# Hybrid retention and S5 step on one core: later ties in the last stage, a later start of retention with joined visits, and the last partial sums added by DMA

## The chip, the cores and the metric

The kernel runs on one core of a Trainium2 chip. A core has a matrix engine (TensorE, here PE, with its weight loads shown apart as PEld), a vector engine (VectorE, DVE), an activation engine (ScalarE, ACT), GpSimd (POOL), a queue engine (SyncE, SP) and 16 DMA engines. Each engine works through its own queue in order. DMAs are issued from the queues of SP, ACT and POOL; an accumulating DMA (one that adds what it reads to what stands at its destination) is issued from POOL. The metric is device time in microseconds (us), the median of several executions. One further execution was recorded by the profiler, and all rows below come from it.

## The reference

One layer of a hybrid decoder, for a prompt of 1024 tokens and 8 sample tokens, in float32, model width 2048:

```python
h = rmsnorm(x, g_pre)
proj = h @ w_in                     # 2048 x 10240
q, k, v, za, ub, zb, ga, gb = split(proj)
ya, s_ret_new = retention(q, k, v, pos, s_ret)       # 8 heads of 128, chunks of 128
ya = (ya * silu(za)) @ w_pa
yb, s_re_new, s_im_new = s5(ub, ...)                 # diagonal state space, gelu, glu gate
yb = (yb * silu(zb)) @ w_pb
merged = sigmoid(ga) * ya + sigmoid(gb) * yb
out = merged @ w_out
return x + rmsnorm(out, g_post), s_ret_new, s_re_new, s_im_new
```

In retention every head has rotated q and k, a decaying state carried over chunks of 128 tokens, scores within a chunk, and a normalization over the head's 128 values. The sample tokens take one step of the same recurrence from a given state.

## The kernel before

**Products.** Activations lie transposed in SBUF, features on the partitions and the 1032 tokens along the free axis. Every float32 operand of a large product is split into a rounded part and a remainder, and a product of two such operands is three matmuls (high by high, high by low, low by high). From the input projection's third pair of row blocks on, the large products go by a Strassen-like scheme: a step (`s`) is a pair of output row blocks and two groups of four k tiles, and has seven products (`n` = 0 to 6) in place of eight. A product (number `g` = 7s + n) is 24 matmuls of 256 to 260 columns pairwise (`product`, L993), or in the out-projection 12 of 324. `prep` makes the weight forms two products ahead (sums on DVE by `add`, L85; the high part on ACT, L974; the remainder on DVE), `evac_st`, `evac_p` and `evac_o` take the sums out of PSUM into the tiles `p1`, `u2`, `u3` (shown as `p`, `u`) and `st`. The steps run in this order: the first part of the input projection, its second half (74 steps in all), the S5 gate (`glu`, 4 steps), the two gated projections `pa` and `pb` (8 each), and the out-projection in two halves of k, `o0` and `o1` (8 each), for tokens 384 to 1031. The scheme needs sums and differences of activation halves; these forms are loaded into `stg` tiles (`stage`, L932) and split (`unstage`, ACT L274 and DVE) by `transition` while the step before still runs.

**Order.** One program order is written out by hand, and a scheduler at compile time puts each engine's instructions into its queue: an instruction goes out when its operands are ready in that schedule, by program order among those that are ready. `tc.issue_after(ins)` holds what is traced in its block behind `ins` in the order of that engine alone on which `ins` runs. `anchor` holds the latest instructions of SP, ACT, DVE and PE. After every product `late_work(g)` runs what was put off with `at(g, ...)`, and `slot()` lets the first background generator of the queue `bg` go on to its next `yield`. One such turn is called a visit.

**Retention** is such a generator (`retention`, L1293). It is put into `bg` at the start of step `C0 + 12` of the input projection, when the pools of the stage before (`k2p`, for reordering the S5 output: tiles `yr`, `yo`) have been closed and the pool `ret` opened in their place. `ret_const` allocates its tiles, fills `mhalf` (-0.5, the exponent of a power that makes the reciprocal root) and loads tables. `head` (L1162) then takes a head in visits: the transposes of v and of the sample tokens' v, which goes out to `vs_d` (L1181) and comes back broadcast as `vb` (L1184); the transposes of k; the state pass, two visits of four matmuls each with four updates on DVE (L1197 to L1205); the sample state; the scores (L1218); the outputs (L1228, L1230); the sample output, a product on DVE and sums over partitions with the small matrices `sel` in two visits (L1239); statistics; the scaling; the transposes back (L1276) and of the sample rows (L1281), and the gating with za. `load_vk` loads the next head's v and k. Between two heads' outputs `mix` makes forms for `pa`.

**Gated projections.** In `pb` the result of a tile is multiplied by its gate (`gated`), and the partial sum that `pa` left in `pap_d` is added. For p = 0 and 1 this is an accumulating DMA into the tile (L1581), and the write to `mg_d` (L1582) is put off by `LAG` = 4 products. For p = 2 to 7 the partial sum is loaded beforehand into a tile `pp` on ACT's queue, DVE adds it, and the tile goes to `mg_d` at once (L1579). `forms_o` reads rows of `mg_d` (L1619) and makes the forms for the out-projection into `fo_d`; its `ld(2)` reads, among others, rows 6 or 14, its `ld(3)` rows 7 or 15.

**The last stage** (L1868 on) is the out-projection of tokens 0 to 383 the other way round, with the tokens on the partitions: three blocks of 128 tokens (c), four column groups of 512 (g), 16 k tiles, three matmuls each (L1874). It counts on in `now`. A group has three banks of PSUM; two of them are halves of one tile, `both_`. In the last group the first 11 k tiles go round the blocks, and then each block does its last five and is taken out by `evac_c`: a sum of squares on ACT (L1845), the product with the norm weights `gb` on DVE (L85), and for the last group the reciprocal root on POOL (L1854), the final scaling with the residual row added (L1857) and the writes of the result (L1858), one for blocks 0 and 1 and three for block 2. `gb` and the residual rows of block 0 (`x_of(0)`) are loaded at steps 9 and 20 of this stage, on POOL's queue, 1 MB each. Beside it run `split_m`, which splits the merged activations of the coming k tiles, and `rows_out`, the norm and the output of the other tokens.

Of the kernel before, what the change touches and what calls it, by code (L numbers as in the profile page):

```python
# [10 lines left out]
F32 = mybir.dt.float32  # L11
F32R = mybir.dt.float32r
I32 = mybir.dt.int32
AF = mybir.ActivationFunctionType
# [65 lines left out]
def emit(ctx, tc, I, O):  # L80
# [80 lines left out]
    rstd = const.tile([128, TOK], F32, name="rstd")  # L161
    warm = const.tile([128, 1], F32, name="warm")
    A.activation(warm, onesk, AF.Square)
    gpre = cload("g_pre", [128, KD])
# [71 lines left out]
    def misc():  # L236
        return banks_of["pms"].tile([128, 512], F32, name="misc")
# [895 lines left out]

    def ret_const():
        K["a"] = act.tile([128, 2, TOK], F32, name="a12")
        K["b"] = act.tile([128, 2, TOK], F32, name="a13")
        vT, kT = K["next"] = R("vT", [128, TOK]), R("kT", [128, TOK], 2)
        P.dma_start(vT, v_d[0])
        yield
        for n, shape in (("col", [128, 4, H]), ("mask", [128, 128])):  # L1140
            K[n] = rp.tile(shape, F32, name=n)
            P.dma_start(K[n], I[n])
        K["mhalf"] = rp.tile([128, 8], F32, name="mhalf")
        V.memset(K["mhalf"], -0.5)
        K["sel"] = rp.tile([128, 2, 32], F32, name="sel")
        P.dma_start(K["sel"].rearrange("p b c -> p (b c)"), I["sel"])
        for a in range(2):
            yield
            P.dma_start(kT[64 * a:64 * a + 64], kq_d[0, 0, a, 0:64])
        yield  # L1150
        yield
# [3 lines left out]
    def load_vk(h):  # L1155
# [4 lines left out]
        return vT, kT  # L1160

    def head(h):  # L1162
        col, mask, mhalf, sel = (K[n] for n in ("col", "mask", "mhalf", "sel"))
# [8 lines left out]
        for i in range(2):  # L1172
# [3 lines left out]
            A.copy(vt[:, 4 * i:4 * i + 4], ps.rearrange("p (c d) -> p c d", c=4))  # L1176
        ps = misc()
        T.transpose(ps[0:8, 0:128], vT[:, SEQ:TOK], ident)
        vs = R("vs", [128, 128])[0:8]
        V.tensor_copy(vs, ps[0:8, 0:128])  # L1180
        P.dma_start(vs_d[h].rearrange("(b d) -> b d", b=8), vs)  # L1181
        yield
# [11 lines left out]
        for i in range(2):  # L1194
            ps = misc()
            for c in range(4):
                T.matmul(ps[:, c * 128:(c + 1) * 128], kt[:, 4 * i + c, :], vt[:, 4 * i + c, :], start=True, stop=True)  # L1197
            for c in range(4):
                n = 4 * i + c
                o = ps[:, c * 128:(c + 1) * 128]  # L1200
                if n == 0:
                    V.tensor_copy(st[:, 0], o)
                else:
                    V.scalar_tensor_tensor(st[:, n], st[:, n - 1], gc, o, ALU.mult, ALU.add)
            yield  # L1205
        P.dma_start(O["retp"][h], st[:, 7])
# [30 lines left out]
        for i in range(2):  # L1237
            for b in range(4):
                T.matmul(ps[32 * b:32 * b + 32, 0:128], sel[:, i, :], pq[:, 4 * i + b], start=i == 0, stop=i == 1,  # L1239
                         tile_position=(0, 32 * b), skip_group_check=True)  # L1240
            if i == 0:
                yield
        ons = R("vs", [128, 128])
# [36 lines left out]
        ps = misc()  # L1280
        T.transpose(ps[:, 0:128], ons, ident)  # L1281
        eb = lambda t: t.rearrange("p (e b) -> p e b", e=2)
        mul(eb(oo[:, SEQ:TOK]), ps[:, 0:128].rearrange("p (b r) -> p r b", r=32)[:, 0:2], eb(za[:, SEQ:TOK]))
# [264 lines left out]
    def load_z(s, name):  # L1548
        kind, p = steps[s]
        r, c = AT[name]  # L1550
        zq[name] = zz_tile()
        A.dma_start(zq[name], {"glu": zy_d, "pa": sga_d, "pb": sgb_d}[kind][2 * p + r, :, HT * c:HT * c + HT])
        if kind == "pb" and p > 1:
            zq[name, "p"] = ppp.tile([128, HT], F32, name="pp")
            A.dma_start(zq[name, "p"], pap_d[2 * p + r, :, HT * c:HT * c + HT])
# [55 lines left out]
    def forms_o(kh, wait):  # L1611
# [14 lines left out]
        for n in range(wait):  # L1626
            yield
            if n == 1:
                ld(2)
# [213 lines left out]
    def evac_c(g, c, ps):  # L1843
# [8 lines left out]
        if g == 3:  # L1852
            V.scalar_tensor_tensor(r1, s4[:, 3:4], 1.0 / D, r1, ALU.mult, ALU.add)
            P.tensor_tensor(r3, r1, r2, ALU.pow)  # L1854
            for i, (a, b) in enumerate(((0, D),) if c < 2 else ((0, 1024), (1024, 1536), (1536, D))):
                z = flat(12 + c, "zc")[:, a:b]
# [5 lines left out]
    for g in range(4):  # L1862
        both_ = banks_of["pst"].tile([128, 2, 512], F32, name="acc")
        ps = [both_[:, 0, :], both_[:, 1, :], mmbank()]
        e = 11 if g == 3 else 13
        todo_ = [[(k, c) for c in range(3)] for k in range(e)] + [[(k, c) for k in range(e, KD)] for c in range(3)]
        for st in todo_:
# [9 lines left out]
            now[0] += 1  # L1877
            if now[0] == lim[0] + 9:
                P.dma_start(gb, bass.AP(tensor=I["g_post_row"].tensor, offset=I["g_post_row"].offset, ap=[[0, 128], [1, D]]))
            if now[0] == lim[0] + 20:  # L1880
                P.dma_start(x_of(0), I["xB"][0])
            if rest:
                with ExitStack() as after:
                    for ins in anchor.values():
                        after.enter_context(tc.issue_after(ins))
                    split_m(rest.popleft())
# [89 lines left out]
```

## Time and profile before

| | us |
|---|---|
| median of 3 executions | 2524.94 |
| lowest and highest of them | 2524.39, 2530.12 |
| the profiled execution | 2526.21 |
| its span, from the first to the last instruction | 2524.4 |

| engine | busy us | share of the span |
|---|---|---|
| PE | 2497.7 | 99% |
| PEld | 2449.6 | 97% |
| DVE | 2011.1 | 80% |
| ACT | 996.8 | 39% |
| POOL | 779.1 | 31% |

How rows of the profile are read: a timeline row gives the start, the duration, the engine, the line of the kernel, the operation, the names of output and inputs (`out<-in`), the shape and the number of like instructions drawn together; in brackets stands how long the engine was idle before it and what ended that. The row of a waits view names who waited for whom, the total, how often, and the longest. A row of the chain gives the start, the duration, the engine, the tile, the line and the count. A row of a window gives its length, the busy time and number of instructions of each engine, the clock that PE was granted, the busy share of the DMA engines and GB/s. Releasers are worked out from semaphores, and one wait for several is put down to the last.

### The profile page before, as it was taken

The numbers are of one execution on the slowest core, as the hardware profiler recorded it, in microseconds if no ns is written. First come the engines' busy times: TensorE is split into PE (matmuls) and PEld (weight loads), VectorE is DVE, ScalarE is ACT, GpSimd is POOL, SyncE is SP. The second block draws the span as 40 slices with busy tenths as digits, with TensorE's granted clock in tenths as the row PEclk, the third lists the DMA queues.
The fourth block names the chain that finished last, engine by engine and source line by source line (L and its number), as shares of the span: only waits on it lengthen the run. The fifth ranks groups of instructions, "written<-read, shape, count | busy, mean of one in ns | idle before, by whom it ended". The sixth has DMA issues, their size and how long they took to land.

```text
span 2524.4 us, 52842 instructions
## 1 busy us (share of the span) xinstructions
PE 2497.7 (99%) x20026; PEld 2449.6 (97%) x20026; DVE 2011.1 (80%) x4212; ACT 996.8 (39%) x1787; POOL 779.1 (31%) x1299
## 2 busy tenths in 40 slices
PE   9999999999999999999999999999999999999998
PEld 8999999999999999999999999999999999999976
DVE  7677789898898898768986766666897878989784
ACT  7143532333333333453334444435552422445532
POOL 0321223222322222223344434444332222433320
PEclk9999999999999999999999999999999999999999
DMA  5879865434434434787889888888888689956883
GB/s 195 282 234 289 231 170 143 139 121 137 131 117 138 135 120 128 244 207 202 223 228 253 225 235 223 211 220 248 270 288 282 226 241 314 304 191 163 220 298 134
DMA packets 242878, 527.59 MB, mean 209 GB/s; under 512 B 42832, under 2 KB 69664, under 8 KB 241856
## 3 DMA queue, kind: packets, MB, share of 16 engines
q0 software_dynamic: 106176, 310.76, 43.1%
q1 hardware_dynamic: 101536, 166.14, 21.1%
q10 hardware_dynamic: 34912, 47.31, 6.0%
q8 instruction: 158, 2.59, 0.4%
q14 instruction: 96, 0.79, 0.1%
HBM read 348.71 MB, written 175.37 MB: 208 GB/s over the span
## 4 chain that ended last, share of the span: by engine, by line
PE 88%; DVE 4%; DMA 3%; issue 3%; POOL 1%; ACT 1%; DVEq 0%; POOLq 0%; ACTq 0%; SPq 0%
PE acc L993 73%; PE acc L1874 4%; PE mm L228 2%; PE mm L229 2%; PE mm L227 2%; DMA u<-pt_d 1%; DMA wr<-in_w_in 1%; DVE u L85 1%; PE misc L825 1%; PE misc L824 1%; DMA wr<-in_w_outB 1%; PE misc L1218 1%; PE misc L1228 1%; PE misc L1197 1%; PE misc L775 1%
## 5 line engine op out<-in xcount | busy, mean ns | idle before, releaser
L993 PE MATMUL acc<-a,whib 128*128 128x256 f32 (+1 forms) x3816 | 629.7, 284 | 4.0 <-DVE u L85 2.3
L993 PE MATMUL acc<-a,whic 128*128 128x256 f32 (+1 forms) x3808 | 629.0, 284 | 2.9 <-DVE u L85 2.3
L993 PE MATMUL acc<-a,whia 128*128 128x256 f32 (+1 forms) x3800 | 627.3, 284 | 0.5 <-ACT whia L974 0.5
L993 PEld LDWEIGHTS acc<-a,whic 128*128 128x128 f32 x3808 | 525.1, 188 | 8.4 <-issue 2.8
L993 PEld LDWEIGHTS acc<-a,whib 128*128 128x128 f32 x3816 | 525.8, 188 | 7.0 <-ACT whia L974 3.9
L993 PEld LDWEIGHTS acc<-a,whia 128*128 128x128 f32 x3800 | 524.3, 188 | 2.7 <-issue 1.4
L993 PE MATMUL acc<-a,wloc 128*128 128x256 f32 (+1 forms) x1904 | 396.4, 283 | 0.4 <-DVE wloc L85 0.4
L993 PE MATMUL acc<-a,wlob 128*128 128x256 f32 (+1 forms) x1908 | 396.8, 283 | 0.0
L993 PE MATMUL acc<-a,wloa 128*128 128x256 f32 (+1 forms) x1900 | 395.2, 283 | 0.0
L993 PEld LDWEIGHTS acc<-a,wloc 128*128 128x128 f32 x1904 | 297.8, 188 | 1.3 <-DVE wloc L85 1.2
L993 PEld LDWEIGHTS acc<-a,wlob 128*128 128x128 f32 x1908 | 298.3, 188 | 0.2
L993 PEld LDWEIGHTS acc<-a,wloa 128*128 128x128 f32 x1900 | 297.1, 188 | 0.0
L974 ACT CAST whic<-wraw 128x512 fp32r<-128x512 f32 x148 | 92.0, 622 | 235.6 <-PE acc L993 157.9
L974 ACT CAST whib<-wraw 128x512 fp32r<-128x512 f32 x146 | 90.7, 622 | 228.7 <-PE acc L993 174.7
L974 ACT CAST whia<-wraw 128x512 fp32r<-128x512 f32 x146 | 90.7, 621 | 221.9 <-PE acc L993 158.9
L85 DVE TENSOR_TENSOR wraw<-wr 128x512 f32<-128x512 f32 x220 | 151.1, 687 | 2.6
L85 DVE TENSOR_TENSOR wloc<-wraw,whic 128x512 fp32r<-128x512 f32 x156 | 107.0, 686 | 50.4 <-ACT whic L974 39.8
L974 ACT CAST whib<-wr 128x512 fp32r<-128x512 f32 x111 | 68.9, 621 | 191.6 <-PE acc L993 155.1
L85 DVE TENSOR_TENSOR wloa<-wraw,whia 128x512 fp32r<-128x512 f32 x154 | 105.6, 686 | 48.2 <-ACT whia L974 32.7
L85 DVE TENSOR_TENSOR a<-stg,a 128x516 fp32r<-128x516 f32 (+1 forms) x224 | 136.2, 640 | 8.4 <-ACT a L274 7.9
L85 DVE TENSOR_TENSOR wlob<-wraw,whib 128x512 fp32r<-128x512 f32 x154 | 105.6, 686 | 46.4 <-ACT whib L974 35.4
L974 ACT CAST whia<-wr 128x512 fp32r<-128x512 f32 x110 | 68.3, 621 | 187.0 <-PE acc L993 159.7
(473 smaller groups left out, 4206.1 us busy)
## 6 DMA issues: line engine op xcount, KB each, us to landing
wr<-in_w_in SPq DMA_DIRECT2D x296, 256.0 KB
pt_d<-u POOLq DMA_DIRECT2D x74, 258.0 KB, 3.4
u<-pt_d POOLq DMA_DIRECT2D x74, 258.0 KB, 5.1
wr<-in_w_out SPq DMA_DIRECT2D x64, 256.0 KB
wr<-in_w_outB SPq DMA_DIRECT2D x64, 256.0 KB
stg<-fm_d POOLq DMA_DIRECT2D x60, 258.0 KB, 4.1
pt_d<-st POOLq DMA_DIRECT2D x37, 258.0 KB, 3.6
pt_d<-p POOLq DMA_DIRECT2D x37, 258.0 KB, 3.1
```

Of the source, the lines that this page charges most:

```text
L85: return (eng or V).tensor_tensor(out, a, b, op)
L227: T.matmul(ps, wh[:, i, :], xh[:, t0:t1], start=first, stop=False)
L228: T.matmul(ps, wh[:, i, :], xl[:, t0:t1], start=False, stop=False)
L229: anchor["p"] = T.matmul(ps, wl[:, i, :], xh[:, t0:t1], start=False, stop=last).ins
L775: T.matmul(ps[:, q * 144:(q + 1) * 144], W1[:, g, :], U[:, g, :], start=True, stop=True)
L824: T.matmul(o, Tm[:, g, :], U[:, g, 0:136], start=True, stop=False)
L825: T.matmul(o, W3[:, g, 1:9, :], X[:, g, 0:136], start=False, stop=True)
L974: anchor["a"] = A.copy(hi, f).ins
L993: anchor["p"] = T.matmul(o, a[:, i, :], x, start=first and i == 0 and a is wh and b is xh, stop=n in (2, 5, 6) and i == 3 and a is wl, ski ...
L1197: T.matmul(ps[:, c * 128:(c + 1) * 128], kt[:, 4 * i + c, :], vt[:, 4 * i + c, :], start=True, stop=True)
L1218: T.matmul(ps[:, c * 128:(c + 1) * 128], kT[:, cs], qT[:, cs], start=True, stop=True)
L1874: anchor["p"] = T.matmul(ps[c], a, b, start=k == 0 and a is xh and b is wh, stop=k == KD - 1 and a is xl).ins
```

## The change

- The tile of one column that ACT's first instruction wrote becomes `mhalf_` of eight columns in the constant pool; DVE then fills it with -0.5, and `ret_const` uses it in place of a tile of its own.
- `ret_const` begins with three empty visits.
- The state pass does both halves in one visit and is followed by two yields. The two sums over `sel` are done in one visit, and the yield between them is gone.
- The sample tokens' v of a head is transposed and written to `vs_d` at the end of the head before (`sample_values`); only the first head does its own.
- For p = 6 and 7 of `pb` the partial sum is added by the accumulating DMA, as for p = 0 and 1, with the write of `mg_d` four products later. `ld(2)` of `forms_o` moves to the last visit of the wait (from the second to the third for `o0`, to the sixth for `o1`).
- In the last stage `gb` and the row loads of block 0 move from steps 9 and 20 to 11 and 24, inside the block that holds instructions behind `anchor`. In the last column group block 1 takes the bank of its own, and block 2 the second half of `both_`. Block 1's final pass and write are split into two halves.

```diff
-    warm = const.tile([128, 1], F32, name="warm")
-    A.activation(warm, onesk, AF.Square)
+    mhalf_ = const.tile([128, 8], F32, name="mhalf")
+    A.activation(mhalf_[:, 0:1], onesk, AF.Square)
+    V.memset(mhalf_, -0.5)
...
     def ret_const():
+        for _ in range(3):
+            yield
...
-        K["mhalf"] = rp.tile([128, 8], F32, name="mhalf")
-        V.memset(K["mhalf"], -0.5)
+        K["mhalf"] = mhalf_
...
+    def sample_values(h, vT, o):
+        T.transpose(o, vT[:, SEQ:TOK], ident)
+        vs = R("vs2", [8, 128])
+        V.tensor_copy(vs, o)
+        P.dma_start(vs_d[h].rearrange("(b d) -> b d", b=8), vs)
...
-        ps = misc()
-        T.transpose(ps[0:8, 0:128], vT[:, SEQ:TOK], ident)
-        vs = R("vs", [128, 128])[0:8]
-        V.tensor_copy(vs, ps[0:8, 0:128])
-        P.dma_start(vs_d[h].rearrange("(b d) -> b d", b=8), vs)
+        if h == HEADS[0]:
+            ps = misc()
+            sample_values(h, vT, ps[0:8, 0:128])
...
                     V.scalar_tensor_tensor(st[:, n], st[:, n - 1], gc, o, ALU.mult, ALU.add)
-            yield
+        yield
+        yield
...
-            if i == 0:
-                yield
         ons = R("vs", [128, 128])
...
         T.transpose(ps[:, 0:128], ons, ident)
+        if h != HEADS[-1]:
+            sample_values(HEADS[HEADS.index(h) + 1], K["next"][0], ps[0:8, 128:256])
...
-        if kind == "pb" and p > 1:
+        if kind == "pb" and 1 < p < 6:
...
-            if n == 1:
+            if n == wait - 1:
                 ld(2)
...
-            for i, (a, b) in enumerate(((0, D),) if c < 2 else ((0, 1024), (1024, 1536), (1536, D))):
+            for i, (a, b) in enumerate((((0, D),), ((0, 1024), (1024, D)), ((0, 1024), (1024, 1536), (1536, D)))[c]):
...
-        ps = [both_[:, 0, :], both_[:, 1, :], mmbank()]
+        ps = [both_[:, 0, :], both_[:, 1, :], mmbank()] if g < 3 else [both_[:, 0, :], mmbank(), both_[:, 1, :]]
...
-            if now[0] == lim[0] + 9:
-                P.dma_start(gb, bass.AP(tensor=I["g_post_row"].tensor, offset=I["g_post_row"].offset, ap=[[0, 128], [1, D]]))
-            if now[0] == lim[0] + 20:
-                P.dma_start(x_of(0), I["xB"][0])
-            if rest:
-                with ExitStack() as after:
-                    for ins in anchor.values():
-                        after.enter_context(tc.issue_after(ins))
+            with ExitStack() as after:
+                for ins in anchor.values():
+                    after.enter_context(tc.issue_after(ins))
+                if now[0] == lim[0] + 11:
+                    P.dma_start(gb, bass.AP(tensor=I["g_post_row"].tensor, offset=I["g_post_row"].offset, ap=[[0, 128], [1, D]]))
+                if now[0] == lim[0] + 24:
+                    P.dma_start(x_of(0), I["xB"][0])
+                if rest:
                     split_m(rest.popleft())
```

## The prediction

> **What bounds the kernel now.** I read the page first, then TensorE's (PE's) waits, then the timelines around its longest gaps, then the chain that ended last, in order of time.
>
> ```profile
> span 2524.4 us, 52842 instructions
> PE 2497.7 (99%) x20026; PEld 2449.6 (97%) x20026; DVE 2011.1 (80%) x4212; ACT 996.8 (39%) x1787; POOL 779.1 (31%) x1299
> ```
>
> PE is busy for 2497.7 of 2524.4 us, so all its idle time together is 26.7 us, start and tail included. No edit takes multiplications away. So a part of the change can win only three things: an idle gap of PE, time that PE spends on switching to other work and back, or the tail after its last matmul. The waits of PE (total, times, longest) say which gaps there are:
>
> ```profile
> PE mm L227 <- ACT whib L220: 5.1, 1, 5.1
> PE acc L993 <- DVE u L85: 4.6, 7, 1.7
> PE acc L993 <- ACT whia L974: 2.1, 4, 0.6
> PE acc L1874 <- DVE wraw L85: 0.8, 1, 0.8
> ```
>
> The 5.1 us is the first load, which the change leaves alone. Of the seven waits for `u`, the evacuation of a product's partial sum, two are long: at 1314.94 (retention begins) and at 2180.59 (the out-projection begins). Both are places that the diff touches.
>
> **The change part by part.** All terms are against the profiled execution.
>
> *Retention begun three steps on, and `mhalf` made at the start.* The timelines of PE, DVE and POOL:
>
> ```profile
> 1314.94 0.71 PE L993 MATMUL acc<-a,whic 128*128 128x256 f32 x4 [1.75 <-DVE u L85]
> 1313.40 0.07 DVE L1144 MEMSET mhalf<- 128x8 f32 x1 [2.75 <-DMA u<-pt_d]
> 1314.11 0.68 DVE L85 TENSOR_TENSOR u<-p,acc 128x516 f32<-128x516 f32 x1
> 1313.80 0.57 POOL L1138 DMA_DIRECT2D vT<-v_d  x1 [4.78 <-DMA fg_d<-yo]
> ```
>
> The DVE stands for 2.75 us in front of a memset of 0.07 us. The view names a transfer into `u`; but a memset reads nothing, and `mhalf` lies in the pool `ret`, opened over the place of `k2p`, whose tile `yo` is still being written out to `fg_d`. POOL's `vT` load was released by that write just then, so I take it for the real releaser. Behind the memset in DVE's queue waits the evacuation of 1314.11, and for that PE, 1.75 us. With `mhalf` in the constant pool, filled long before, this DVE wait cannot occur. Three steps on is 3 x 2.82 = 8.5 us later (a product's 2.82 is in the rows below), more than the 4.78 that POOL waits now, so that wait goes too. Late next is the ordinary evacuation, for which PE doesn't wait elsewhere in this stage. Gain: 1.75 and a slower restart (0.71 for four matmuls where the next four take 0.63), **1.8 us**; bounds 1.5 to 2.0. The new memset waits for the Square in the same tile at the start; the 5.1 us of the first load cover both.
>
> *Visits joined.* A retention step ("visit") puts its matmuls between two products. The chain in order of time shows a head (start, us, group):
>
> ```profile
> 1334.18 2.86 PE acc L993 x24
> 1337.94 2.87 PE acc L993 x24
> 1341.70 5.69 PE acc L993 x48
> 1347.39 1.78 PE misc L1218 x16
> 1349.17 2.82 PE acc L993 x24
> 1355.34 5.65 PE acc L993 x48
> 1361.35 3.06 PE acc L993 x24
> 1364.76 8.75 PE acc L993 x72
> ```
>
> A product that no visit precedes takes 2.82. The state pass's two visits lie between the first three rows: 1337.94 - 1337.04 = 0.90 and 1341.70 - 1340.81 = 0.89. The scores (L1218) do twice as many matmuls in one visit of 1.78, so joining doesn't shorten the matmuls; only one of two surcharges of 0.05 on the next product goes: 0.05 a head, **0.4 us** in eight (0 to 0.6). The second visit isn't dropped, it becomes empty. The two sums over `sel` (L1239, eight records each) are the gaps before 1361.35 and 1364.76: 0.36 and 0.35, and the product between takes 3.06, a surcharge of 0.24. This yield is dropped. The joined visit costs between 0.36 (the second half runs in the shadow of the first) and 0.71 (nothing saved inside), so a head wins 0.24 to 0.59; I take 0.36, since of a visit so short I put a third, 0.12, down to going there and back. Eight heads: **2.9 us**, bounds 1.9 to 4.7. A head's visits fall from 14 to 13, and retention ends 3 - 8 = 5 visits earlier, where nothing waits for it on PE.
>
> *Sample values moved into the head before.* One transpose, one copy and one DMA per head change place. Before, POOL wrote `vs_d` and its next load, of `vb`, stood until that had landed; now seven of eight heads spare most of this wait. But over the eight heads (busy PE, PEld, DVE, ACT, POOL behind the length of the window)
>
> ```profile
> 1331.00:1717.00 386.00, 386.00 (x3336) 379.81 (x3335) 258.39 (x571) 164.80 (x314) 161.75 (x242) 1.00 0.86 226
> ```
>
> PE is busy all of 386.00 us at a granted clock of 1.00: what POOL waits for here is hidden, and I cost the edit at **0** (0 to -0.5). What hides the moved transpose's input is the next head's `vT` load, issued when `sel` is done, four visits before it, both before and after.
>
> *Last partial sums by transfer.* For p = 6 and 7 of the second gated projection, eight loads of `pp` on ACT's queue and eight DVE additions go; eight accumulating DMAs and eight later writes of `mg_d` come to POOL, as p = 0 and 1 have them already.
>
> The same view at the end of that projection, and the timelines behind it:
>
> ```profile
> 2150.00:2175.00 25.00, 25.00 (x206) 25.00 (x205) 24.86 (x47) 14.18 (x30) 13.35 (x25) 1.00 0.92 306
> ```
>
> ```profile
> 2172.35 0.69 DVE L85 TENSOR_TENSOR u<-u,pp 128x516 f32<-128x516 f32 x1
> 2173.34 0.54 POOL L1579 DMA_DIRECT2D mg_d<-u  x1 [0.56 <-DVE u L85]
> 2173.87 0.54 POOL L932 DMA_DIRECT2D stg<-fo_d  x1
> 2178.95 0.50 DVE L85 TENSOR_TENSOR a<-stg,a 128x324 fp32r<-128x324 f32 x1 [1.40 <-ACT a L274]
> 2180.59 0.54 PE L993 MATMUL acc<-a,whib 128*128 128x324 f32 x2 [1.54 <-DVE u L85]
> ```
>
> Here DVE is busy for 24.86 of 25.00 us, and the additions are part of that, 0.69 each: 5.5 us in eight. The last one holds back POOL's write (0.56), behind it stands a load of `stg`, which lands late, DVE waits 1.40 for its split, and PE 1.54. Without the additions DVE comes to the out-projection without its backlog: up to the 1.5 us of this gap are won, and as much again in what runs late behind it, 3.0. Against it stand the waits of POOL for the same pair of DMAs at p = 0 and 1 (waits of POOL from 2005 to 2080), and those of reads behind writes of `mg_d` (waits of the whole run):
>
> ```profile
> POOL mg_d L1582 <- DMA u<-pap_d: 13.3, 4, 5.3
> POOL mg_d L1582 <- DMA st<-pap_d: 9.6, 2, 5.0
> POOL mg_d L1582 <- DMA p<-pap_d: 9.1, 2, 5.6
> ```
>
> ```profile
> POOL a L1619 <- DMA mg_d<-u: 15.6, 4, 6.7
> ```
>
> That is 32.0 us in eight waits, 4.0 each, with everything on POOL queued behind. At p = 0 and 1 little was queued; at p = 7 it is the 28 loads of the out-projection's first operands, on six buffers. If the waits are spread, the six buffers cover them; if one falls in front of the last four loads, PE pays about its 4.0. So bounds -3.0 and +4.0, and I take **0**, between them, as relief and delay meet in the same loads. The later `ld(2)` is read seven visits after its issue and costs nothing. [...]
>
> *Last stage: later `gb` and row loads.*
>
> ```profile
> 2372.89 0.74 POOL L1881 DMA_DIRECT2D a<-in_xB  x1
> 2383.41 0.51 ACT L274 CAST a<-a 128x384 fp32r<-128x384 f32 x1 [4.27 <-DMA a<-mg_d]
> 0.84 0.12 DVE L1851 MEMSET small<- 128x1 f32 x3
> ```
>
> The 1 MB row load is written at step 20 of the stage and yet issued at 2372.89, before its first matmul; ACT then waits 4.27 for a load issued behind it, and PE the 0.8 of L1874 above. The last row shows why I expect this to stay: a memset of the last stage runs at 0.84, so instructions go out as soon as they can, not where they are written. The new tie holds instructions behind the latest ones of SP, ACT, DVE and PE, on those same engines; these two DMAs are on POOL. **0**, bounds 0 and -1.0.
>
> *Last stage: the banks and the split write of the second row block.* One row of the chain, then DVE's timeline at the end:
>
> ```profile
> 2441.40 69.80 PE acc L1874 x303
> ```
>
> ```profile
> 2508.19 2.35 DVE L1857 SCALAR_TENSOR_TENSOR a<-a,small,a 128x2048 f32<-128x2048 f32 x1 [0.70 <-POOL small L1854]
> 2511.94 0.69 DVE L85 TENSOR_TENSOR a<-acc,a 128x512 f32<-128x512 f32 x1 [1.39 <-ACT misc L1845]
> 2513.36 2.35 DVE L1857 SCALAR_TENSOR_TENSOR a<-a,small,a 128x2048 f32<-128x2048 f32 x1 [0.67 <-POOL small L1854]
> 2515.63 0.68 DVE L85 TENSOR_TENSOR a<-acc,a 128x512 f32<-128x512 f32 x1
> 2517.04 2.61 DVE L1857 SCALAR_TENSOR_TENSOR a<-a,small,a 128x1024 f32<-128x1024 f32 x3 [0.66 <-POOL small L1854]
> ```
>
> A matmul is 69.80/303 = 0.23 us, and a block's last five k tiles are 15 of them, 3.5 us. Block 1 shared a PSUM tile with block 0, whose evacuation it had to let pass, and PE ran part of block 2 first: its DVE product is at 2511.94. With its own tile it is ready 3.5 after block 0's; DVE is then free at 2508.19 + 2.35 = 2510.54. Its final pass starts 1.42 later (2513.36 - 2511.94), at 2511.96, and ends at about 2514.4, where block 2's product starts instead of at 2515.63. Gain **1.2 us**; bounds 0 (the order stays) and 2.1 (block 2's product, ready at about 2513.5, goes between the two halves).
>
> Sum: 1.8 + 0.4 + 2.9 + 1.2 = 6.3 us off a span of 2524.4, so 2518.1. The profiled execution took 2526.21, 1.8 beyond its span and 1.3 above the median of 2524.94; I take the difference off the median: **2518.6 us**.
>
> **The rivals.** (1) *DVE's relief wins at the out-projection*: for it DVE's 24.86 of 25.00, against it POOL's 32.0. The 3.0 are won: 2518.6 - 3.0 = 2515.6; if the tie also holds the row load, 2514.6. (2) *The new period turns against the products.* Today 14 visits make a head, exactly two weight steps of seven products, and no head has a PE wait; with 13 each head meets the weight sums and evacuations on DVE elsewhere. If half the heads pay the 0.6 of one DVE operation in front of an evacuation, 2.4 goes: 2521.0. Against it, DVE is busy for only 258.39 of 386.00 us here. (3) *POOL's waits delay the loads*: the +4.0, 2522.6. (4) *Slower than before*: the last four `stg` loads stand behind two writes of `mg_d` and behind the read of the row that these write. Price: both waits for `p`, 9.1, and the longest read, 6.7, are 15.8, less the 1.5 of today's gap, which they replace: 2518.6 + 14.3 = 2532.9. It decides from the point where POOL's order puts the read for `ld(2)` ahead of these loads; from a wait of 7.8 (6.3 and the 1.5) the kernel is slower than before. (5) *The joined sums save nothing*, both halves and the surcharge staying: 2521.5.
>
> **How the numbers follow.** Forecast 0.38, (1) 0.24, (2) 0.13, (3) 0.13, (4) 0.06, (5) 0.06. 0.3% is 7.6 us, about what a measurement can tell from no change; that bound is 2517.4. Below it lie most of (1), 0.21, and a third of the forecast, 0.12: faster 0.33. Slower by as much is (4), 0.06. The rest, 0.61, is within. The bounds added up, -1.5 -0 -1.9 +4.0 at one end and -2.0 -0.6 -4.7 -0.5 -3.0 -1.0 -2.1 at the other, give +0.6 and -13.9, or 2525.5 and 2511.0; they don't fall together, and leaving out 2 in 10 I take 2513.0 to 2523.5.
>
> **What would show it.** Right: no DVE memset and no PE gap where retention begins; one group of 16 records for the joined sums in each head, and heads 13 products apart instead of 14; the last DVE pass starting near 2510.7 on a span of 2518. Wrong: PE gaps between heads, POOL idle for a `pap_d` landing in front of `stg` loads with PE gaps over 1.5 at the out-projection, or the row load issued well inside the last stage with ACT no longer waiting. The prediction falls if the joined sums save outside 0.24 to 0.59 a head, or if queue orders far from the touched places change and bring gaps of their own.

## The result and the profile after

| | before | after |
|---|---|---|
| median of 20 executions each, us | 2524.82 | 2530.28 |
| lowest and highest | 2521.75, 2530.12 | 2526.99, 2534.98 |
| profiled execution | 2526.21 | 2531.0 |
| its span | 2524.4 | 2529.2 |

The ratio is 1.002, with a 95% interval of 1.0013 to 1.0027. The change costs 5.5 us where 6.3 were to be saved, and the time lies above the range.

The page of the kernel after, its span and the busy time of the engines:

```profile
span 2529.2 us, 52812 instructions
...
PE 2496.8 (99%) x20026; PEld 2452.1 (97%) x20026; DVE 2008.7 (79%) x4205; ACT 997.3 (39%) x1787; POOL 785.8 (31%) x1307
```

PE's busy time stayed (2497.7 before), so its idle time grew from 26.7 to 32.4 us. The waits of PE after (total, times, longest) show by which groups:

```profile
PE acc L994 <- DVE u L85: 7.4, 8, 3.1
...
PE acc L994 <- ACT a L275: 2.3, 1, 2.3
```

The wait for `u` has one more case than before, and its longest is 3.1 in place of 1.7. The 2.3 for `a` (the split of a loaded operand form) is new. To see where the time comes in, I put the start of the same matmul in both traces side by side:

| first matmul of | before | after | difference |
|---|---|---|---|
| a product 24 us ahead of the wait at 1314.94 | 1290.44 | 1290.04 | -0.4 |
| the product that had waited 1.75 there | 1314.94 | 1312.63 | -2.3 |
| a product just behind retention | 1747.98 | 1744.55 | -3.4 |
| a product at the end of `pb` | 2158.73 | 2155.63 | -3.1 |
| the last stage | 2374.2 | 2379.5 | +5.3 |
| end of the span | 2524.4 | 2529.2 | +4.8 |

Up to the end of `pb` the changed kernel is ahead. Within the next 35 us it loses 8.4 us. PE's timeline after, its rows with a wait in that stretch:

```profile
2162.35 0.72 PE L994 MATMUL acc<-a,whia 128*128 128x256 f32 x4 [0.91 <-DVE u L85]
...
2167.71 0.71 PE L994 MATMUL acc<-a,whib 128*128 128x256 f32 x4 [2.26 <-ACT a L275]
...
2178.72 0.56 PE L994 MATMUL acc<-a,whic 128*128 128x324 f32 x2 [1.05 <-DVE u L85]
...
2185.60 0.70 PE L994 MATMUL acc<-a,whib 128*128 128x324 f32 x2 [3.07 <-DVE u L85]
```

That is 7.3 us of waiting; before, the same stretch had 1.54 and one of 0.52. The missing 3 us stand in the column of the granted clock, here in windows of 2 us (length, PE busy, matmuls, clock, DMA share, GB/s):

```profile
2166.00:2168.00 2.00, 0.29 (x2) 1.00 1.04 269
2168.00:2170.00 2.00, 2.00 (x14) 0.68 0.74 271
2170.00:2172.00 2.00, 2.00 (x11) 0.50 0.60 190
2172.00:2174.00 2.00, 2.00 (x15) 0.96 0.91 188
...
2184.00:2186.00 2.00, 0.40 (x2) 0.95 1.01 381
2186.00:2188.00 2.00, 2.00 (x10) 0.50 1.03 386
2188.00:2190.00 2.00, 2.00 (x11) 0.70 0.96 312
```

After each of the two longest waits PE runs at half its clock for some 3.4 us and so loses another 1.7: (0.32 + 0.50 + 0.04) x 2 and (0.05 + 0.50 + 0.30) x 2. Waits 7.3 - 2.0 = 5.3, clock 3.4: 8.7, about the 8.4 lost.

What PE waits for is seen on POOL, in its timeline of the same kernel:

```profile
2143.75 0.54 POOL L1589 DMA_DIRECT2D mg_d<-st  x1 [5.13 <-DMA st<-pap_d]
...
2150.02 0.55 POOL L1589 DMA_DIRECT2D mg_d<-u  x1 [3.72 <-DMA u<-pap_d]
...
2152.22 1.83 POOL L933 DMA_DIRECT2D stg<-mg_d  x2
2156.43 0.55 POOL L1589 DMA_DIRECT2D mg_d<-p  x1 [2.38 <-DMA p<-pap_d]
2160.03 0.54 POOL L1589 DMA_DIRECT2D mg_d<-u  x1 [3.06 <-DMA u<-pap_d]
2160.57 2.13 POOL L933 DMA_DIRECT2D stg<-fo_d  x4
...
2169.55 0.55 POOL L1589 DMA_DIRECT2D mg_d<-st  x1 [4.84 <-DMA st<-pap_d]
2170.08 1.07 POOL L933 DMA_DIRECT2D stg<-fo_d  x2
```

The late write of `mg_d` stands on POOL for the landing of the accumulating DMA, though it was put off by four products in the program's order. The loads of `stg` written behind it stand too: between 2154 and 2160.57 none goes out, and four then go at once. ACT's timeline shows the next link, the splitting of such a load:

```profile
2165.52 0.91 ACT L275 CAST a<-stg 128x324 fp32r<-128x324 f32 x2 [3.94 <-DMA stg<-fo_d]
```

DVE makes the remainder behind it (idle 2.49 ahead of 2166.02, the trace has it as a wait for ACT's `a`), and the evacuation queues behind that on DVE. PE waits for the evacuation three times, and once, the 2.26, for ACT's split itself.

### The profile page after: what moved, and what is told of

The parts are those of the page before. It is cut to its first block, busy times and chain, and to the rows that moved or that the text cites. A ratio compares the mean times of both kernels' runs of the same rounds, so it can differ in the third digit from the quotient of the medians.

```text
span 2529.2 us, 52812 instructions
## 1 busy us (share of the span) xinstructions
PE 2496.8 (99%) x20026; PEld 2452.1 (97%) x20026; DVE 2008.7 (79%) x4205; ACT 997.3 (39%) x1787; POOL 785.8 (31%) x1307
## 5 line engine op out<-in xcount | busy, mean ns | idle before, releaser
L994 PEld LDWEIGHTS acc<-a,whib 128*128 128x128 f32 x3816 | 527.5, 189 | 11.6 <-issue 4.6
L975 ACT CAST whic<-wr 128x512 fp32r<-128x512 f32 x109 | 67.7, 621 | 180.2 <-PE acc L994 156.5
```

Of the source, the lines that this page charges most:

```text
L975: anchor["a"] = A.copy(hi, f).ins
L994: anchor["p"] = T.matmul(o, a[:, i, :], x, start=first and i == 0 and a is wh and b is xh, stop=n in (2, 5, 6) and i == 3 and a is wl, ski ...
```

## The experiments

Theory A: the transfers in place of the additions cost about 8 us, through POOL's order. Rival B: the new period of the retention visits, or another order elsewhere, delays that stage. Rival C: the added transfers cost by their bytes, wherever they stand. The runs were made on several chips, so each is set against the kernel before on its own chip, ratios alone are compared between chips, and single stages are read from traces. Where a run is one execution alone (five to nine), its time is not compared: the starts of the same matmuls, by their place in PE's order, are set side by side instead.

**One: the additions back, all else changed.**

```diff
-        if kind == "pb" and 1 < p < 6:
+        if kind == "pb" and p > 1:
...
-            if n == wait - 1:
+            if n == 1:
                 ld(2)
```

This edit and the next also move `ld(2)`; the third run leaves it late and loses nothing, so it isn't the cause.

> The changed kernel with one part undone: the partial sums of the last two steps of the second block of columns are added on VectorE again, and the third load of the output forms stands where it stood. Theory A (the transfers cost about 8 us, because the merged writes behind them wait in POOL's queue for a landing and the loads of the out-projection stand behind the writes): about 2522, some 8 us under the changed kernel and 2.5 to 3 under the kernel before; no wait of TensorE over 1 us between 2150 and 2190. Rival B (the new period of the retention visits, or another order elsewhere, pushes that stage late): 2528 or more, and the waits between 2150 and 2190 stay.

Measured: 2527.39 (2523.21 to 2531.49, 12 executions) beside 2530.25 of the kernel before, a ratio of 0.9993 (0.9982 to 1.0003). The changed kernel had 1.002, so the part is worth some 0.27%, 6.8 us. From the end of `pb` to the last stage this run takes what the kernel before takes (the products there are 0.5 us later at the end than at the beginning), and PE's waits are 1.9 and 0.5, as the kernel before has them with 1.5 and 0.5; that none would be over 1 us was missed. B falls. The gain over the kernel before is 1.8 and no more than its interval allows; this profiled execution lost time at 215 to 222 and at 1344, places that this edit doesn't touch.

**Two: the transfers alone, on the kernel before.** The reverse of the edit above.

> The kernel before with nothing but the transfers in place of the last two steps' additions and the later third load. Theory A: 2532 to 2534, 8 us over the kernel before, with the waits of TensorE behind the second block of columns that the changed kernel shows. Rival B: 2525, no change. My prediction said 2522 to 2529 (-3.0 to +4.0), with 2525 as the likeliest.

Measured: 2539.61 beside 2530.25, 1.0036 (1.0024 to 1.0048), 9.1 us slower, with waits of PE of 1.0, 2.8, 0.8 and 3.8 between 2167 and 2192. The transfers alone make more than the whole loss.

**Three: the transfers kept, their writes out of the loads' way.** The write is held behind the load of `stg` that POOL issued last when it is traced:

```diff
-        eng.dma_start(r, src)
+        tied[eng is P] = eng.dma_start(r, src).ins
...
-            at(g + LAG, lambda: P.dma_start(mg_d[m, :, cols], t))
+            at(g + LAG, lambda: put(mg_d[m, :, cols], t))
...
+def _put(tc, P, tied, o, t):
+    with tc.issue_after(tied[True]):
+        P.dma_start(o, t)
```

> The changed kernel, all its transfers kept, but each merged write that waits for a landing is tied behind POOL's newest load of the operand stages, so that fewer loads stand behind a waiting write. TensorE's, ScalarE's and SyncE's orders are those of the changed kernel. Theory A: most of the 8 us comes back, 2522 to 2525. Rival C (the transfers' bytes and the memory traffic are the cost, wherever they stand): 2530, as the changed kernel. Rival B: 2530 too.

Measured: 2527.39 beside 2530.25, 0.9987 (0.9977 to 0.9998). POOL's timeline of this run, at the place of the rows above:

```profile
2149.60 1.42 POOL L933 DMA_DIRECT2D stg<-mg_d  x2
2150.67 0.88 POOL L1987 DMA_DIRECT2D mg_d<-u  x1
2152.20 1.07 POOL L933 DMA_DIRECT2D stg<-fo_d  x2 [0.65 <-DVE a L85]
2153.26 0.55 POOL L1987 DMA_DIRECT2D mg_d<-p  x1
```

The same transfers and bytes, but the writes come when their tiles have landed, and the loads go out when their buffers come free. Between 2137 and 2170 the writes of `mg_d` wait 0.5 us for landings, where they waited 19.1 in the changed kernel. PE's order is the same, and still its four waits shrink to one, of 2.97 at 2178.53. C falls, and the mechanism of A is shown: not the transfers cost, but a wait at the head of POOL's queue.

**Four: the transfers at another place.** On the kernel before, `p in (2, 3, 6, 7)` keeps the additions, so that p = 4 and 5 have the transfers.

> The kernel before with as many more transfers as the change adds, but at the fifth and sixth step of the second block of columns and not at the last two, where the loads of the out-projection stand behind; the later third load as in the changed kernel. Theory A: the place decides, 2523 to 2527. Rival C (each added transfer costs, wherever it is): about 2533.

Measured: 2540.67, 1.0047 (1.0031 to 1.0064), 11.9 us slower. That part of A falls: the place doesn't save it. C's number is near, but the third run has ruled C out, and POOL's waits (2100 to 2190; total, times, longest) show A's mechanism here too:

```profile
POOL mg_d L1582 <- DMA st<-pap_d: 12.2, 2, 6.2
POOL mg_d L1582 <- DMA u<-pap_d: 8.7, 3, 6.7
```

At p = 4 and 5 the writes of `fo_d` and the first loads of `stg` stand behind these waits, and PE waits 4.99 at 2171.10, more than at any place of the changed kernel.

**Five to eight: the other terms, one execution each, on the tied kernel of the third run** (which leaves all of them in). First the sums over `sel` in two visits again (`if i == 0: yield` put back):

> The changed kernel with its merged writes tied as in the run before, and the sums over the samples' state parted over two visits again. Measured on the trace: how much later the products stand at the end of retention, counted from the product ahead of retention, against the tied kernel (which there is 1.75 us earlier than the kernel before, retention's later start not counted). Theory J (the joined sums save 0.45 us times 16 less 0.66 times 8, 1.9 us, which my prediction put at 2.9, and the transposes of the normalised output give some of it back for the new place that the shorter period puts them at): the splitting costs 1.9 and the transposes' 2.6 us of excess go, so the end of retention moves by -0.7 to +0.5 us. Rival K (the transposes wait for a reason of their own, the moved sample values or the state pass): it moves by +1.9 and the transposes' excess stays.

The stretch from a product ahead of retention to one some 40 us behind it takes 490.5 us in place of 485.0, 5.5 more: both theories miss. Of it, 4.3 are a wait of 2.58 in the last head, at 1735.23, with 1.7 of half clock behind it, and 0.5 is a wait of the first head. Without these 0.7 is left, between J's upper end of 0.5 and K's 1.9. The distances of the products show what it is made of. In a head the three products around the sums take 9.66 us with two visits and 9.24 to 9.29 with one, which is 3.3 in eight heads, so J's 1.9 for the splitting was too small. Against it the transposes lose 3.0 of excess in the first seven heads (J had 2.6): the three products around them take 10.5 in each, where the tied kernel has 11.75, 11.2 and 11.7 in the first, second and seventh. J's mechanism holds, its price for the sums does not, and the wait in the last head is missing in it; run nine shows where it is from.

The state pass over two visits again:

```diff
-        yield
-        yield
+            yield
```

> The same tied kernel with the state pass over two visits again, the number of visits unchanged. My prediction priced the joining at 0.4 us saved (0 to 0.6): the end of retention 0.4 us later, one more entry of eight matmul groups (8 times some 0.05). If the joined pass is what makes the transposes wait (one form of rival K): their excess of 2.6 us goes, and the end of retention is 2 us earlier.

0.3 us longer over the same stretch; the transposes are as slow as before (11.6 in the row that has 11.5 after). My 0.4 held.

The sample tokens' v back at the head's first visit (`sample_values` called there in every head, and not at the end of the head before):

> The same tied kernel with the samples' values transposed at the head's first visit again, instead of beside the transposes at the end of the head before. My prediction put the move at 0 (0 to 0.5 saved). From the traces: the eight transposes at the head's beginning cost 1.16 us of excess in the kernel before; theory: undone, the end of retention is 1.0 to 1.2 us later. Rival K: the transposes at the head's end lose their excess (0.5 to 2.6 us), and the end of retention is as early or earlier.

4.7 us longer. 2.1 of it is a wait at 1339, of the first head, whose code is the same in both. What comes back in every head that the edit touches is some 0.25 us at its beginning, less 0.1 spared at the end of the head before: 1.1 in seven heads, as the theory had it. The transposes at the end keep their excess, so K falls. The rest is mainly a wait of 0.9 at 1551, which costs 1.3 with what follows and which one execution can't put down to the edit. So the move is worth 1.1, and 2.4 if that wait belongs to it. I had 0 to 0.5.

The old banks, and block 1's output in one piece:

```diff
-        ps = [both_[:, 0, :], both_[:, 1, :], mmbank()] if g < 3 else [both_[:, 0, :], mmbank(), both_[:, 1, :]]
+        ps = [both_[:, 0, :], both_[:, 1, :], mmbank()]
```

> The same tied kernel with the last group's accumulators in the old order of banks and the middle block's output written in one piece. My prediction priced the two at 1.2 us saved (0 to 2.1). Measured from the last product of the out-projection's second half to the span's end: 1.2 us longer than with them if that holds; the same if the last block's own passes set the end either way.

DVE's timeline at the end, after and then in this run:

```profile
2517.42 2.48 DVE L1864 SCALAR_TENSOR_TENSOR a<-a,small,a 128x1024 f32<-128x1024 f32 x2 [0.67 <-POOL small L1861]
...
2521.22 2.61 DVE L1864 SCALAR_TENSOR_TENSOR a<-a,small,a 128x1024 f32<-128x1024 f32 x3 [0.66 <-POOL small L1861]
```

```profile
2515.34 2.35 DVE L1864 SCALAR_TENSOR_TENSOR a<-a,small,a 128x2048 f32<-128x2048 f32 x1 [0.67 <-POOL small L1861]
...
2519.01 2.61 DVE L1864 SCALAR_TENSOR_TENSOR a<-a,small,a 128x1024 f32<-128x1024 f32 x3 [0.66 <-POOL small L1861]
```

PE's last matmul starts at 2517.93 and at 2514.58. From there to the last pass: 3.29 with the edit, 4.43 without. It saves 1.14; my 1.2 held. As the expectation measured it, from the last product of the out-projection to the span's end, this run takes 151.5 and the tied kernel 150.3. In the pair of before and after 0.5 of it reaches the span's end: from the last matmul's start 11.8 and 11.3, since from the last pass to the end it takes 7.4 before and 8.0 after.

**Nine: the start alone, on the kernel before.**

> The kernel before with nothing but the retention begun three steps on and the constant for the power made at the start. My prediction: 1.8 us saved (1.5 to 2.0) at the product where TensorE waited 1.75 us at 1315, nothing after it. If the later start costs at the other end of retention (the last head's visits meeting the next stage), the products behind retention stand less than 1.8 us ahead of the kernel before, or behind it.

2525.93, one execution, beside a median of 2525.75 (2522.43 to 2529.29), which can't tell 1.8 us. In the trace no wait is left at 1315, and the product there is 1.9 earlier; but the product behind retention is 0.6 later than in the kernel before. PE's and ACT's timelines at the last head show where it went:

```profile
1734.24 0.33 PE L1278 MATMUL misc<-ident,kT 128*128 128x128 f32 x1 [2.58 <-ACT kT L1271]
```

```profile
1733.69 3.19 ACT L1271 ACTIVATE kT<-kT,nb,rsd 128x128 f32<-128x128 f32 x8 [2.56 <-DVE nb L1268]
```

Three steps later, the last head's transposes come at the same time as the activations that feed them, and these wait for `nb` on DVE. With the joined sums retention ends earlier and the wait is gone: after, PE has no wait over 0.5 us there. So the later start alone wins nothing, and the run with the sums split again paid this same 2.58. The joined sums without the later start were not run.

**Ten and eleven: the two rows of the last stage truly held back.** `tied["m"]`, POOL's latest load of merged rows, joins the instructions behind which they stand, once with the transfers (their writes tied) and once with the additions back:

```diff
-                for ins in anchor.values():
+                for ins in (*anchor.values(), tied["m"]):
                     after.enter_context(tc.issue_after(ins))
```

> The tied kernel (all of the change, merged writes behind POOL's newest stage load) with the row of post-norm weights and the residual row of the last stage held behind POOL's newest load of merged rows as well, so that they do move. Theory: only two waits of TensorE of 0.2 to 0.7 us at the last stage's beginning can come from those rows, so this run is 0 to 1 us under the tied kernel, which stands at 0.9987 of the kernel before: 0.998 to 0.999. Rival: the rows delay the merged loads by more than the waits show, 0.997 or less.

> The changed kernel with the additions of the last two steps on VectorE again, and the two rows tied as in the run beside it. Against that run it tells whether the transfers, once their writes stand out of the loads' way, gain anything over the additions. Theory A: VectorE's relief (eight additions of some 0.6 us) lies under TensorE's products, so both runs agree within 2 us. Rival (relief decides, as one case of my prediction had it): the transfers' run is 4 us or more faster.

Measured beside 2525.75 of the kernel before: with the transfers 2520.83, 0.9984 (0.9975 to 0.9993); with the additions 2520.08, **0.9976 (0.9967 to 0.9985)**, the fastest version. In the changed kernel the row load went out at 2378.19, ahead of the stage's first matmul at 2379.5. POOL's timeline of the fastest version:

```profile
2379.83 0.53 POOL L1889 DMA_DIRECT2D a<-in_g_post_row  x1
2380.35 0.53 POOL L1891 DMA_DIRECT2D a<-in_xB  x1
```

The stage begins at 2368.6 there, so the row goes out 11.8 us into it. The stage's longest group of matmuls (min, median, max ns, first and last start) after, and in this version:

```profile
L1881 PE MATMUL acc<-whia,a x126: 387/389/505, 2379.5 to 2517.2; 128*128 128x512 f32 x126
```

```profile
L1881 PE MATMUL acc<-whia,a x126: 387/389/504, 2368.6 to 2503.7; 128*128 128x512 f32 x126
```

137.7 against 135.1 us: 2.6 saved, where I had at most 1.0 (with the transfers 1.4, from 136.5 to 135.1; with the additions 3.0, from 138.1). PE has no wait over 0.15 us left in this stage. The first expectation's 0.998 to 0.999 held for the whole time. Between the two versions lie 0.0008, 2.0 us, in favour of the additions, and their intervals overlap: theory A holds, VectorE's relief gains nothing that can be measured here. The other version has a wait of PE of 2.83 where the out-projection begins; this one has 1.03.

**Twelve: an empty visit moved**, to free the transposes:

```diff
                     V.scalar_tensor_tensor(st[:, n], st[:, n - 1], gc, o, ALU.mult, ALU.add)
         yield
-        yield
...
         A.activation(ons, ons, AF.Identity, scale=rs[:, 8:9], bias=nb[:, 8:9])
+        yield
         yield
```

> The version without the transfers and with the two rows tied (0.9976 of the kernel before), with one empty visit of each head moved: from behind the state pass to between the normalising activations and the transposes that read them. The number of visits stays. Theory J: the transposes' excess of 2.6 us between 1345 and 1745 goes, since ScalarE's eight activations (3.2 us) are then done when the transposes come; the run is 1.5 to 2.7 us under that version, near 0.9966. Rival: the output pass, now one visit closer to the state pass, waits for VectorE's states instead; no gain, 0.997 to 0.999.

Measured: 2534.19 beside 2530.7, 1.0014 (1.0002 to 1.0026). PE's groups from 1345 to 1745 (busy, mean ns, idle before):

```profile
L1224 PE MATMUL misc<-a,kT 128*128 128x128 f32 x128 | 18.3, 294 | 7.7 <-DVE a L1210 7.7
```

The transposes' excess went, as said (9.6 busy in place of 11.5), but the scores, now one visit closer to the state pass, wait 7.7 us for the state's updates on DVE (L1210). Two stretches of half clock behind these waits, at 1362 and at 1414, add 1.7 each. The rival holds in its mechanism, though it named the outputs and not the scores, and it was worse than its 0.997 to 0.999: the empty visit was needed.

## Why the prediction was wrong, point by point

The signs of being right for retention came: no memset and no wait where it begins, one group of 16 records for the sums, heads 13 products apart. So did a sign of being wrong: POOL idle for landings of `pap_d` in front of `stg` loads, with PE's gaps over 1.5 at the out-projection.

- **What bounds the kernel.** Right that only PE's idle time, its switching and the tail can be won. Wrong in taking a microsecond of idling for a microsecond: two waits cost 1.7 more each.
- **Retention begun later.** Held at its place: -1.9 at the product that had waited (-2.3 less the -0.4 of the product ahead), 1.8 predicted. "Where nothing waits for it on PE" doesn't hold for the start alone, which gives 2.58 back in the last head; with the joined sums it does.
- **Visits joined.** Both terms held: 0.3 for the state pass, where I had 0.4, and 3.3 for the sums, where I had 2.9. The sums save 0.36 to 0.42 a head, inside the 0.24 to 0.59 with which the prediction was to stand or fall. PE's timelines of before and after show it in the second head, by the first matmuls of the product ahead of the sums and of the third product after it, 9.66 and 9.23 apart:

```profile
1408.90 0.64 PE L993 MATMUL acc<-a,whib 128*128 128x256 f32 x4
...
1418.56 0.63 PE L993 MATMUL acc<-a,whib 128*128 128x256 f32 x4
```

```profile
1413.64 0.64 PE L994 MATMUL acc<-a,whia 128*128 128x256 f32 x4
...
1422.87 0.64 PE L994 MATMUL acc<-a,whia 128*128 128x256 f32 x4
```

  What failed is that the sum has no term for the new period. PE's groups from 1345 to 1745, before and after:

```profile
L1276 PE MATMUL misc<-ident,kT 128*128 128x128 f32 x64 | 9.8, 273 | 0.0
...
L1239 PE MATMUL misc<-vT,sel 128*32 128x128 f32 x128 | 6.8, 285 | 0.0
```

```profile
L1281 PE MATMUL misc<-ident,kT 128*128 128x128 f32 x64 | 11.5, 280 | 0.8 <-ACT kT L1274 0.5
...
L1246 PE MATMUL misc<-vT,sel 128*32 128x128 f32 x128 | 5.2, 279 | 0.0
```

  The transposes of the normalised outputs take 1.7 more and wait 0.8. (The sums' own busy time falls by 1.6 alone; the distance between the products, which falls by 3.3, also has the time that PE spends on going there and back.) The reason is in the timelines of ACT and PE after:

```profile
1376.19 3.18 ACT L1274 ACTIVATE kT<-kT,nb,rsd 128x128 f32<-128x128 f32 x8
```

```profile
1376.87 1.35 PE L1281 MATMUL misc<-ident,kT 128*128 128x128 f32 x4
```

  The four transposes start 0.7 us into the 3.18 of the activations that they read, and take 1.35; before, they took 0.60, with the activations begun 2.0 us earlier (1371.38, transposes at 1373.35). That is the first head. By the distances of the products the same happens in the second and the seventh, where the transposes start 0.6 and 0.7 into the activations; in the others they start 2.2 us in or later and cost 0.1 more than before, for the sample transpose that has moved there. The three heads lose 3.0 together. This is the second rival's idea, a new period that meets other work, at about its price of 2.4; but PE meets ACT's activations and no evacuation. With the value of the next term: 3.3 + 0.3 + 1.1 - 3.0, less a wait of 0.7 in the first head, is 1.0. Between the product at retention's start and the one behind it the changed kernel wins 1.1, where 3.3 were to come.
- **Sample values moved.** Costed at 0 because PE was busy; but a busy PE was also switching. Worth 1.1, or 2.4 with a wait that may be chance.
- **Last partial sums by transfer: the step that failed.** "I take 0, between them, as relief and delay meet in the same loads", with +4.0 as the worst. It cost 8.4 in the changed kernel, 9.1 alone. The relief was nothing: with the writes out of the way PE still waits 2.97, since ACT waits there for `stg` loads (2.60 ahead of 2173.70, 1.15 ahead of 2176.57) and DVE for ACT. The delay was no single wait of 4.0: POOL's five waits for landings from 2137 to 2170 sum to 19.1 (5.13 + 3.72 + 2.38 + 3.06 + 4.84), each with the next loads behind it, the six buffers cover only part, and PE pays four times and then runs at half clock. I had such waits in hand (32.0 at p = 0 and 1). The third rival, with a chance of 0.13, had this mechanism at the price of one wait, 4.0. The fourth had the sign and the place, but priced it at 14.3, by a read of `mg_d` that isn't what held the loads back: in the changed kernel no such read waits more than 0.5 there.
- **Rows of the last stage.** Right that the tie holds nothing (2378.19, ahead of the stage). The bound of 1.0 for a tie that holds was too small: 1.4 to 3.0.
- **Banks and split write.** Right: 1.14 for 1.2 at the last pass, of which 0.5 reached the span's end in this pair.

Together, from the table: -0.4 ahead of retention, -1.9 at retention's start, -1.1 in retention, +0.3 up to the end of `pb`, +8.4 by the transfers and -0.5 at the end are the +4.8 of the span.

Open stay small differences between executions: waits at 215 to 222 (0.4 before and after, over 4 in the first run of the experiments), of the first head at 1337 to 1344 (0 to 2.1) and of 1.36 at 1918 after come and go between executions, and their cause wasn't tried.

## What to carry to other kernels

A DMA that must wait for another DMA's landing belongs behind everything on its queue that could go now (here 19.1 us of such waits became 0.5): count not its own lateness but all that is queued behind it, and check in the scheduled order where it really stands. Parts of a change that shift the same background work are priced together, at both ends of the shift and at each place that the shifted work meets. What a visit costs is read from the distance of the products around it, not from its own busy time (3.3 us and 1.6 for the sums). An edit that is inert shows nothing of its idea: make it hold once before dropping it.

## What the runs showed of the hardware

A wait of PE can cost more than it lasts, and its length alone doesn't tell whether it does. After the waits of 2.26 and 3.07 above PE was granted half its clock for 3.4 us; after the wait of 2.97 in the tied kernel it was not. The same wait of 2.58 in the last head was followed by half clock in the run with the sums split, and not in the run with the start alone.

Here are PE's windows around these two waits of 2.58 (length, PE busy, matmuls, clock, DMA share, GB/s), with the sums split and with the start alone:

```profile
1732.00:1734.00 2.00, 0.65 (x6) 1.00 0.88 121
1734.00:1736.00 2.00, 0.77 (x6) 0.97 0.41 144
1736.00:1738.00 2.00, 2.00 (x11) 0.50 0.44 54
1738.00:1740.00 2.00, 2.00 (x15) 0.68 0.49 87
```

```profile
1730.00:1732.00 2.00, 1.66 (x14) 1.00 0.44 27
1732.00:1734.00 2.00, 0.00 (x0) 1.00 0.94 237
1734.00:1736.00 2.00, 1.76 (x15) 1.00 0.00 0
1736.00:1738.00 2.00, 2.00 (x19) 1.00 0.96 114
```

In the first run 1.7 is lost behind the wait, (0.03 + 0.50 + 0.32) x 2; in the second nothing. So it is around the wait of 2.97 in the tied kernel:

```profile
2174.00:2176.00 2.00, 1.56 (x11) 1.00 1.07 291
2176.00:2178.00 2.00, 0.00 (x0) 1.00 1.00 380
2178.00:2180.00 2.00, 1.47 (x10) 1.00 1.02 394
2180.00:2182.00 2.00, 1.99 (x13) 1.00 1.01 363
```

Shorter waits part as well. In the twelfth run the one of 1.83 at 1413.24 is followed by half clock (0.90, 0.50 and 0.75 in the windows of 2 us from 1412 to 1418), and behind the one of 1.85 at 1343.61 the clock stays at 1.00. About the end of the wait of 3.8 in the second run the clock was low for longer than behind the others: 0.62, 0.50, 0.50 and 0.68 in the windows from 2190 to 2198, which makes 6.8 us at half clock. What parts the waits that are followed by half clock from those that aren't was not tried in a run of its own. So a wait of some 2 to 3 us costs here its length and, if half clock follows, 1.7 more; which of the two holds is read from the clock behind it in that trace.
